# Four more modulation sixths summed on VectorE, and expert weights loaded as 8 KB rows

## The chip, the cores and the metric

The kernel runs on one core of a Trainium2 chip. The metric is the device time of one execution in microseconds. The kernel before takes 947.39 us (median of three executions, 945.4 to 949.32).

## The reference

Two layers work on 256 latent tokens and 256 context tokens of width 1024. Layer 0 mixes by latent attention beside a gated linear recurrence, layer 1 by a Hyena operator with long filters. Each layer is modulated by the conditioning and ends in a mixture of 16 experts, two of them per token. All weights are float32.

```python
for layer in range(DEPTH):
    mod = (silu_c @ ada_w[layer] + ada_b[layer])[:, None, :]
    sh1, sc1, g1, sh2, sc2, g2 = jnp.split(mod, 6, axis=-1)
    h_lat = modulate(rms_norm(x, norm1_g[layer]), sh1, sc1)
    ...
    x = x + g1 * o_lat
    h_lat = modulate(rms_norm(x, norm2_g[layer]), sh2, sc2)
    ...
    x = x + g2 * grouped_moe(h_lat, router_w, router_b, w1, w3, w2)
# grouped_moe, for each expert e of 16
act = jax.nn.silu(h @ w1[e]) * (h @ w3[e])
y = y + gates[..., e:e + 1] * (act @ w2[e])
```

`ada_w[layer]` is 1024 x 6144, so each of the six "sixths" of a layer is a product of a vector of 1024 with a 1024 x 1024 matrix.

## The kernel before, in words

All weights pass through one list of tiles, each 128 partitions x 2048 floats (1 MB). The list is planned at the start (`plan`, `plan_ada`, `moe_tiles`) and loaded in that order by SyncE (`emit`, the load at L219) into a ring of nine buffers `w`, eight buffers `sp` that the mixers also use for their activations, and one to three buffers `x`. A load waits until its buffer's last reader is done. Each of the two mixtures runs over seven passes (`PASSES`): six with two experts and one with four. In a pass the products with w1 and w3 (`up`, L1244) and w2 (`down`, L1272) take most of TensorE's time; between them stand transposes of the activations (`turn`, L1259) and the scatter back to the tokens (`back`, L1289).

A tile of w1 or w3 holds 512 rows of 512 floats: row r of the matrix lies in partition r mod 128, so each partition gets four pieces of 2 KB. A tile of w2 gives each partition two pieces of 4 KB (2 KB for the last pass, whose w2 comes in column halves).

The sixths of the modulation are made in the background by `ada_step`, one of eight row blocks per step, called from the mixer's hand-written sequence `SEQ`, from the attention's list `ATT` and elsewhere. `PLAN` says for each sixth (layer, number) who forms its two column halves. "V" is VectorE: one multiply (L449) and seven multiply-adds over 128 x 512 (L451). "P" is TensorE: eight products with the conditioning as 32-column weights (L442), four at a time in column groups, and a copy on ScalarE (L446). Without an entry a sixth is "VP", one half on each. A finished sixth is turned into columns four steps later (`ada_columns`, transposes at L372, sums at L379 or L381), or into a row spread over the partitions (`ada_row`, L391).

In front of a mixture the router transposes the tokens (`enter`, L576), ScalarE and VectorE write the normalized tokens as a high and a low part (`high`, L627, and `low_`, L633), and TensorE gathers the tokens of each expert from these (L1204, L1215).

The order of each engine's instructions is made by the framework's scheduler from the program order and from its own timing estimates; within the mixtures a few stretches are left as written.

Of the kernel before, what the change touches and what calls it, by code (L numbers as in the profile page):

```python
# [24 lines left out]
STATIC = 4  # L25
DYN = 16 - STATIC
PASSES = ((0, 1), (2, 3), (8, 9), (4, 5, 6, 7), (10, 11), (12, 13), (14, 15))
LAST = len(PASSES) - 1
QUAD = 4
NW = 9  # L30
N8 = 8
# [29 lines left out]
FILLS = 40  # L61
PLAN = {(0, 3): "VV", (1, 2): "VV", (1, 4): "PP", (1, 5): "PP"}
TIN = 0
# [30 lines left out]
def _pack_params(v):  # L94
    pk = np.zeros((128, NPK), np.float32)

    def cols(name, a):
        a = np.asarray(a)
        pk[:a.shape[0], PK[name]:PK[name] + a.shape[1]] = a

    def chunks(a):
        return np.asarray(a).reshape(-1, 128).T

    cols("c", chunks(v["c"]))
    cols("cc", chunks(v["c_ctx"]))
    cols("n1", chunks(v["norm1_g"]))
    cols("n2", chunks(v["norm2_g"]))
# [10 lines left out]
    cols("rw", np.asarray(v["router_w"]).reshape(8, 128, 16).transpose(1, 0, 2).reshape(128, 128))  # L118
    cols("adab", chunks(v["ada_b"]))
# [47 lines left out]
def build(tc, A, dbg=None, stop=None):  # L167
# [43 lines left out]
    def emit(n):  # L211
        for _ in range(n):
            if emitted[0] < len(order):
# [4 lines left out]
                v = t[:shape[0], :shape[1] * shape[2]].rearrange("p (k f) -> p k f", k=shape[1])  # L218
                nc.sync.dma_start(v, src() if callable(src) else src)  # L219
                made[key] = v  # L220
# [51 lines left out]

    def expert(nme, l, e, r0, nk, c0, nf):

        w = A["moe_" + nme]
        if e < STATIC:
            return mat(w[l, e], r0, nk, c0, nf)
        return lambda: mat(w[l, bass.ds(chosen[l][e - STATIC], 1)].rearrange("o k f -> (o k) f"), r0, nk, c0, nf)

    def moe_tiles(l):  # L280
        for j, es_ in enumerate(PASSES):
            for nme in ("w1", "w3"):
                for kk in range(2):
                    for e in es_:
                        yield ((nme, l, e, kk), expert(nme, l, e, kk * 512, 4, 0, 512), (128, 4, 512))
            for h in range(2):
                for e in es_:
                    if j < LAST:
                        yield (("w2", l, e, h), expert("w2", l, e, h * 256, 2, 0, 1024), (128, 2, 1024))
                    elif h == 0:  # L290
                        yield (("w2", l, e, 0), expert("w2", l, e, 0, 4, 0, 512), (128, 4, 512))
            if j == LAST:
                for h in range(2):
                    for e in es_:
                        yield (("w2", l, e, 1 + h), expert("w2", l, e, h * 256, 2, 512, 512), (128, 2, 512))

# [71 lines left out]
    def ada_columns(l, s, hf, use, e, four, n):  # L368

        p2 = ps()  # L370
        for m in range(4):
            T.transpose(p2[:, m * 128:m * 128 + 128], e[:, m * 128:m * 128 + 128], ident)  # L372
        pv = p2.rearrange("p (m q r) -> p m q r", m=4, q=4)
# [165 lines left out]
    def in_order(engines=""):  # L539
# [3 lines left out]
        if engines:  # L543
            manual.append(tc.manual_schedule(engines={ENG[e] for e in engines}))
            manual[0].__enter__()

    class router:

# [22 lines left out]
        def enter(self, i):  # L571
# [3 lines left out]
            for k in range(4):  # L575
                T.transpose(p[:, k * 128:k * 128 + 128], x[:, t, (4 * n + k) * 128:(4 * n + k) * 128 + 128], ident)  # L576
            S.activation(self.alloc().bitcast(BF16)[:, :512], x[:, t, n * 512:n * 512 + 512], AF.Square,
# [45 lines left out]
        def high(self, t):  # L623

            for n in range(2):
                c = slice(n * 512, n * 512 + 512)
                S.activation(self.y[0][:, t, c], x[:, t, c], AF.Copy, scale=self.r[t])  # L627

        def low_(self, t):

            for n in range(2):
                c = slice(n * 512, n * 512 + 512)
                V.scalar_tensor_tensor(self.y[1][:, t, c], x[:, t, c], self.r[t], self.y[0][:, t, c].bitcast(F32),  # L633
                                       op0=OP.mult, op1=OP.subtract)

# [525 lines left out]
    def moe(l, route, ws, filler=None, fills=((0, 0, 0),) * 8, budget=0, late=None, prepare=None, finish=None):  # L1161
# [94 lines left out]
        def turn(j):  # L1256
            p = ps()
            for k in range(4):
                T.transpose(p[:, k * 128:k * 128 + 128], act[j][:, k * 128:k * 128 + 128], ident)  # L1259
            at = act[j] = w2("at")  # L1260
# [53 lines left out]
        def again(nme, e, k, n=0):  # L1314
            t = wk.tile([128, 512], F32, tag="t2", name=nm("wr"), bufs=WT2[l])
            nc.sync.dma_start(t, A["moe_" + nme][l, e, k * 128:k * 128 + 128, n * 512:n * 512 + 512])
            return t
# [9 lines left out]
        next(steps, None)  # L1327
        bg_all()
        route.gates()
# [8 lines left out]
        for j in range(LAST + 1):  # L1338
# [8 lines left out]
            else:  # L1347
                slots(0, gate, firsts)
                slots(1, gate, firsts)
            fill(fills[j][0])  # L1350
            up(j, "w3", first, firsts)
# [421 lines left out]
```

## Time and profile before

| | |
|---|---|
| median of three executions | 947.39 us |
| the profiled execution's own time | 945.29 us |
| its span, first to last instruction | 943.4 us |
| granted TensorE clock, mean | 0.975 |
| TensorE busy | 863.5 us (92%) |
| VectorE busy | 462.8 us (49%) |
| ScalarE busy | 228.9 us (24%) |
| read from HBM | 287.42 MB, 306 GB/s over the span |

Shares of busy time are averages over stages: start (to 45 us), mixer of layer 0 (to 250), mixture 0 (to 530), Hyena mixer (to 690), mixture 1 (to 933) and the end. In the rows PE is TensorE's matrix multiply and PEld its weight load, DVE VectorE, ACT ScalarE, SP SyncE. One float32 product of the program appears in the records as two MATMULs. A busy TensorE isn't one at its peak, since the ends of its instructions are modelled.

### The profile page before, as it was taken

To read this page: it belongs to the slowest core of one execution; us is meant where nothing else is said; L and a number is where in the kernel's file an instruction comes from. 1 tells how busy PE (TensorE), PEld (TensorE's weight loads), DVE (VectorE), ACT (ScalarE), POOL (GpSimd) and SP (SyncE) were. 2 spreads that over 40 slices of the span, in tenths; PEclk is the share of its full clock that TensorE was granted. 3 is DMA by queue.
4 is the path that set the end of the run, shared out by engine and by line. 5 is a ranking of instruction groups with operands and counts; after the bars stand their busy time and mean duration, and the time that the engine had idled before them with its cause. 6 is when DMAs were issued, how large, how long until landed. Compare 5 with 4: busy or idle time off the path is not lost. (4 is left out here: it accounts for less than half of the span.)

```text
span 943.4 us, 10841 instructions
## 1 busy us (share of the span) xinstructions
PE 863.5 (92%) x3976; PEld 447.2 (47%) x3976; DVE 462.8 (49%) x1124; ACT 228.9 (24%) x446; POOL 15.7 (2%) x21
## 2 busy tenths in 40 slices
PE   3998999999999999899998599999989999988984
PEld 2345655574553534333433487776553532423431
DVE  5469785771643454536433648756272323122123
ACT  3276414430411221313122222211031110100112
POOL 0000000000000010101000000000000000000000
PEclk9999999999899999999999799999979999999998
DMA  9957689476799999999999673643199999999993
GB/s 351 353 187 248 224 269 369 165 248 242 244 385 397 329 384 387 395 390 396 396 338 372 229 267 131 223 151 116 57 386 352 389 395 387 404 389 396 396 387 144
DMA packets 130567, 289.33 MB, mean 307 GB/s; under 512 B 6828, under 2 KB 8876, under 8 KB 130500
## 3 DMA queue, kind: packets, MB, share of 16 engines
q1 hardware_dynamic: 129428, 286.39, 82.9%
q10 hardware_dynamic: 1072, 2.10, 0.7%
q8 instruction: 36, 0.59, 0.3%
q14 instruction: 31, 0.25, 0.1%
HBM read 287.42 MB, written 1.05 MB: 306 GB/s over the span
## 5 line engine op out<-in xcount | busy, mean ns | idle before, releaser
L1244 PE MATMUL ps<-w,xe 128*64 128x512 f32 (+1 forms) x696 | 174.6, 597 | 2.4 <-DMA w<-in_moe_w 2.4
L1244 PEld LDWEIGHTS ps<-w,xe 128*64 128x64 f32 (+1 forms) x696 | 50.4, 129 | 87.5 <-issue 79.2
L1272 PE MATMUL ps<-w,at 128*64 128x512 f32 (+1 forms) x344 | 86.0, 597 | 4.5 <-DMA w<-in_moe_w 2.7
L1594 PE MATMUL ps<-xt,w 128*128 128x256 f32 x384 | 87.4, 388 | 1.8 <-ACT xt L1558 1.8
L1594 PEld LDWEIGHTS ps<-xt,w 128*128 128x128 f32 x384 | 74.4, 195 | 14.6 <-ACT xt L1558 2.1
L1291 DVE TENSOR_TENSOR x<-x,ps 128x512 f32<-128x512 f32 x56 | 36.9, 683 | 64.6 <-PE ps L1289 64.6
L1278 DVE SCALAR_TENSOR_TENSOR ye<-ps,gs,grow 128x512 f32<-128x512 f32 x28 | 20.9, 748 | 83.1 <-PE ps L1272 83.1
L1244 PE MATMUL ps<-sp,xe 128*64 128x512 f32 (+1 forms) x216 | 54.5, 598 | 1.4 <-DMA sp<-in_moe_w 1.2
L451 DVE SCALAR_TENSOR_TENSOR e<-w,sg,e 128x512 f32<-128x512 f32 x70 | 51.4, 744 | 3.0 <-DMA w<-in_ada_w 2.3
L1272 PEld LDWEIGHTS ps<-w,at 128*64 128x64 f32 (+1 forms) x344 | 26.7, 130 | 50.6 <-issue 40.0
L1280 ACT ACTIVATE yeh<-ye 128x512 fp32r<-128x512 f32 x28 | 17.6, 630 | 117.5 <-DVE ye L1278 117.5
L1244 PE MATMUL ps<-x,xe 128*64 128x512 f32 (+1 forms) x112 | 37.4, 595 | 1.6 <-DMA x<-in_moe_w 1.6
L1254 DVE TENSOR_TENSOR th<-th,ps 128x512 f32<-128x512 f32 x14 | 9.6, 687 | 59.0 <-PE ps L1244 59.0
L1244 PEld LDWEIGHTS ps<-sp,xe 128*64 128x64 f32 (+1 forms) x216 | 16.7, 132 | 30.0 <-issue 26.3
L1220 ACT ACTIVATE xe<-ps,modc 128x256 f32<-128x256 f32 (+1 forms) x32 | 15.8, 539 | 58.0 <-DVE xe L1218 58.0
L517 PE MATMUL ps<-w,x 128*128 128x512 f32 x64 | 28.4, 595 | 0.7 <-ACT x L1608 0.7
L1249 ACT ACTIVATE th<-ps 128x512 f32<-128x512 f32 x14 | 8.4, 597 | 84.1 <-PE ps L1244 68.5
L835 PE MATMUL ps<-hT,w 128*128 128x512 f32 x64 | 28.0, 593 | 0.4 <-DMA w<-in_ev_w_in 0.4
L517 PE MATMUL ps<-w,mix 128*128 128x512 f32 x64 | 28.2, 594 | 0.0
L1272 PE MATMUL ps<-sp,at 128*64 128x512 f32 (+1 forms) x112 | 26.0, 598 | 2.3 <-ACT at L345 1.7
L442 PE MATMUL ps<-w,cs 128*32 128x512 f32 x160 | 27.1, 714 | 0.0
L930 PE MATMUL ps<-w,hT 128*128 128x288 f32 (+1 forms) x96 | 26.8, 434 | 0.0
(355 smaller groups left out, 1311.0 us busy)
## 6 DMA issues: line engine op xcount, KB each, us to landing
w<-in_moe_w SPq DMA_DIRECT2D x126, 1024.0 KB, 13.9
w<-in_ada_w SPq DMA_DIRECT2D x48, 1024.0 KB, 7.3
sp<-in_moe_w SPq DMA_DIRECT2D x41, 1024.0 KB, 14.6
x<-in_moe_w SPq DMA_DIRECT2D x21, 1024.0 KB, 14.2
w<-in_od_w_in SPq DMA_DIRECT2D x12, 1024.0 KB, 6.8
w<-in_ev_w_in SPq DMA_DIRECT2D x4, 1024.0 KB, 10.9
w<-in_ev_w_out SPq DMA_DIRECT2D x4, 1024.0 KB, 7.9
w<-in_moe_w SPq DMA_DIRECT2D x8, 512.0 KB, 9.8
```

The costliest lines, as they stand in the source:

```text
L442: T.matmul(part[hf][32 * q:32 * q + 32, :], cs[:, k - 3 + q, :], get(("ada", l, s, hf, k // 4))[:, q, :], start=(k == 3), stop=(k == 7), t ...
L451: V.scalar_tensor_tensor(eh, w[hf], c, eh, op0=OP.mult, op1=OP.add)
L517: T.matmul(po[t][n], a[:, k, t * 128:t * 128 + 128], b[:, n * 512:n * 512 + 512], start=(k == korder[0] and i == 0), stop=(k == korder[-1] ...
L835: T.matmul(uxp[b], get(("wux", hf))[:, k % 4, b * 128:b * 128 + 128], hT[hf][:, k % 4, :], start=(k == 0), stop=(k == KD - 1))
L930: T.matmul(p[:, :n], hT[k // 4][:, k % 4, t * 128:t * 128 + 128], get((w, k // 4))[:, k % 4, :], start=(k == 0), stop=(k == KD - 1))
L1220: S.activation(e[:, k, :w], p[:, w:2 * w], AF.Identity, scale=sc[:, k:k + 1], bias=sh[:, k:k + 1])
L1244: T.matmul(p[room * i:room * i + room, :], xe[j // 2][:, k, o:o + room], weight(nme, e, k), start=(k == 0), stop=(k == KD - 1), tile_posit ...
L1272: T.matmul(p[room * i:room * i + room, :], act[j][:, o:o + room], weight("w2", e, k, n), start=(k == 0), stop=(k == 3), tile_position=(0, ...
L1278: V.scalar_tensor_tensor(e, po[j, n], gs[j], grow[l, 5][:, n * 512:n * 512 + 512], op0=OP.mult, op1=OP.mult)
L1280: S.activation(h, e, AF.Copy)
L1291: V.tensor_tensor(xs, xs, p, op=OP.add)
L1594: T.matmul(pb, w[:, k % 4, b * 128:b * 128 + 128], hT[:, k, :], start=(k == 0 and b % 2 == 0), stop=(k == KD - 1 and b % 2 == 1))
```

## The change

It has three parts. `PLAN` now gives both halves of the sixths (0, 2), (0, 4), (0, 5) and (1, 0) to VectorE; before they were "VP". The expert tiles are cut otherwise: a partition takes consecutive rows of the matrix, four of w1 and w3, two of w2, which are 8 KB without a gap (`GROUP`, `expert_rows`). The last pass's w2, a column half, keeps rows of 2 KB, and its tile of four becomes two loads. So that the sums stay the same, everything that meets these tiles is permuted: norm2's gains, the router's weights and the second halves of the biases on the host, the router's transposes and the modulation's column transposes of sixths 3 to 5 with a stride of four floats, the high and low parts read with a stride of four, and `turn` with a stride of two. Last, the call that finishes the open background work (`bg_all`) moves in each mixture from ahead of the gates to behind the first pass's `slots`.

```diff
+GROUP = {"w1": 4, "w3": 4, "w2": 2}
...
-PLAN = {(0, 3): "VV", (1, 2): "VV", (1, 4): "PP", (1, 5): "PP"}
+PLAN = {(0, 2): "VV", (0, 3): "VV", (0, 4): "VV", (0, 5): "VV", (1, 0): "VV", (1, 2): "VV", (1, 4): "PP", (1, 5): "PP"}
...
-                nc.sync.dma_start(v, src() if callable(src) else src)
+                a = src() if callable(src) else src
+                if len(a.shape) == 3:
+                    nc.sync.dma_start(v, a)
+                else:
+                    g = a.shape[2]
+                    for b in range(a.shape[1]):
+                        nc.sync.dma_start(v[:, b * g:b * g + g], a[:, b])
...
+    def expert_rows(w, nme, c0, nf):
+        return w.rearrange("(a p k) f -> p a k f", p=128, k=GROUP[nme])[:, :, :, c0:c0 + nf]
...
-            T.transpose(p2[:, m * 128:m * 128 + 128], e[:, m * 128:m * 128 + 128], ident)
+            T.transpose(p2[:, m * 128:m * 128 + 128], e[:, m * 128:m * 128 + 128] if s < 3 else e[:, m::4], ident)
...
-                T.transpose(p[:, k * 128:k * 128 + 128], x[:, t, (4 * n + k) * 128:(4 * n + k) * 128 + 128], ident)
+                T.transpose(p[:, k * 128:k * 128 + 128], x[:, t, n * 512 + k:n * 512 + 512:4], ident)
...
-                S.activation(self.y[0][:, t, c], x[:, t, c], AF.Copy, scale=self.r[t])
+                S.activation(by_rows(self.y[0][:, t, c]), x[:, t, c].rearrange("p (q k) -> p k q", k=4), AF.Copy,
+                             scale=self.r[t])
...
-                V.scalar_tensor_tensor(self.y[1][:, t, c], x[:, t, c], self.r[t], self.y[0][:, t, c].bitcast(F32),
-                                       op0=OP.mult, op1=OP.subtract)
+                V.scalar_tensor_tensor(by_rows(self.y[1][:, t, c]), x[:, t, c].rearrange("p (q k) -> p k q", k=4),
+                                       self.r[t], by_rows(self.y[0][:, t, c].bitcast(F32)), op0=OP.mult, op1=OP.subtract)
...
-                T.transpose(p[:, k * 128:k * 128 + 128], act[j][:, k * 128:k * 128 + 128], ident)
+                T.transpose(p[:, k * 128:k * 128 + 128], act[j][:, k // 2 * 256 + k % 2:k // 2 * 256 + 256:2], ident)
...
         next(steps, None)
-        bg_all()
         route.gates()
...
                 slots(1, gate, firsts)
+                bg_all()
             fill(fills[j][0])
```

The table shows little of what moves. On VectorE in the mixer, between the features of the queries and the copy of the queries (`qm`), this stands in the kernel before; `e` is the sum of a sixth, `w` a weight tile, `y` the recurrence's gate:

```order
L449 TENSOR_SCALAR e_861<-w_862,sg 128x512
L451 SCALAR_TENSOR_TENSOR e_777<-w_811,sg,e_777 128x512
L451 SCALAR_TENSOR_TENSOR e_861<-w_862,sg,e_861 128x512
L343 COPY vt_708<-ps_855 128x256
L422 SCALAR_TENSOR_TENSOR e_777<-fixed_71,kc,e_777 24x512
L451 SCALAR_TENSOR_TENSOR e_861<-w_862,sg,e_861 128x512 x2
L451 SCALAR_TENSOR_TENSOR e_861<-w_902,sg,e_861 128x512 x4
L422 SCALAR_TENSOR_TENSOR e_861<-fixed_71,kc,e_861 24x512
L974 TENSOR_SCALAR y_99<-y_99 128x1024
L975 TENSOR_TENSOR y_99<-y_99,ug_366 128x1024
L1070 SCALAR_TENSOR_TENSOR y_99<-y_99,ug_366 128x1024
L343 COPY qm_907<-ps_913 128x384
```

And this in the changed kernel, whose lines 467, 438, 994, 995, 1090 and 359 are lines 451, 422, 974, 975, 1070 and 343 of before:

```order
L467 SCALAR_TENSOR_TENSOR e_857<-w_860,sg,e_857 128x512
L438 SCALAR_TENSOR_TENSOR e_775<-fixed_71,kc,e_775 24x512
L467 SCALAR_TENSOR_TENSOR e_857<-w_858,sg,e_857 128x512
L994 TENSOR_SCALAR y_99<-y_99 128x1024
L467 SCALAR_TENSOR_TENSOR e_857<-w_860,sg,e_857 128x512
L467 SCALAR_TENSOR_TENSOR e_857<-w_897,sg,e_857 128x512
L995 TENSOR_TENSOR y_99<-y_99,ug_366 128x1024
L467 SCALAR_TENSOR_TENSOR e_857<-w_860,sg,e_857 128x512
L467 SCALAR_TENSOR_TENSOR e_857<-w_897,sg,e_857 128x512
L467 SCALAR_TENSOR_TENSOR e_857<-w_899,sg,e_857 128x512
L1090 SCALAR_TENSOR_TENSOR y_99<-y_99,ug_366 128x1024
L359 COPY qm_903<-ps_909 128x384
```

The sums of the sixths (0, 2) and (0, 5), `e_775` and `e_857` there, have doubled and now also stand between the gate's steps and ahead of the copy of the queries. In all, 24 of the added operations stand ahead of VectorE's first softmax maximum (L1084 before) and eight between it and the attention's last output (L1113).

On TensorE, where the keys and values (L1004) wait for VectorE's features of the queries, this stands before; L442 are the products of the sixth (0, 2):

```order
L372 MATMUL ps_789<-kc,e_547 128x128 x4
L372 MATMUL ps_797<-kc,e_547 128x128 x4
L442 MATMUL ps_806<-w_784,cs 32x512 x2
L1004 MATMUL ps_749<-w_556,cT_724 128x512
L1004 MATMUL ps_754<-w_556,cT_724 128x512
L442 MATMUL ps_806<-w_784,cs 32x512 x2
L442 MATMUL ps_806<-w_813,cs 32x512 x4
L958 MATMUL ps_818<-kc,cqn_774 128x128
```

In the changed kernel (lines 388, 1024 and 978 are 372, 1004 and 958):

```order
L388 MATMUL ps_790<-kc,e_547 128x128 x4
L388 MATMUL ps_798<-kc,e_547 128x128 x4
L1024 MATMUL ps_747<-w_556,cT_722 128x512
L1024 MATMUL ps_752<-w_556,cT_722 128x512
L978 MATMUL ps_817<-kc,cqn_772 128x128
```

The eight products are gone, as in three more places of the mixer, and the transposes of `cqn` stand right behind the work that waits for nothing new.

On SyncE the loads keep their order but for a few buffers; each expert tile, `128x4x512` or `128x2x1024` before, is one load of `128x2048`, and each layer has four loads more, for the last pass's w2.

## Rows read from the trace of the kernel before

**Rows 1.** The page: busy us and share of each engine
```profile
PE 863.5 (92%) x3976; PEld 447.2 (47%) x3976; DVE 462.8 (49%) x1124; ACT 228.9 (24%) x446; POOL 15.7 (2%) x21
```
**Rows 2.** Stretches: start:end, length, busy per engine (count), clock, DMA share, GB/s
```profile
100.00:167.00 67.00, 67.00 (x289) 39.84 (x288) 49.60 (x126) 20.39 (x43) 0.00 (x0) 1.00 0.84 298
167.00:213.00 46.00, 44.75 (x294) 29.60 (x292) 35.48 (x85) 19.47 (x47) 0.00 (x0) 1.00 0.59 204
...
250.00:530.00 280.00, 258.60 (x1249) 111.67 (x1242) 129.31 (x336) 61.88 (x126) 13.71 (x16) 0.98 1.02 378
700.00:930.00 230.00, 213.16 (x1022) 85.79 (x1021) 64.01 (x142) 28.81 (x58) 0.00 (x0) 0.99 1.01 382
```
**Rows 3.** Waits of TensorE, whole span: for whom, us in total, times, longest
```profile
PE ps L1272 <- DMA w<-in_moe_w: 2.7, 4, 0.7
...
PE ps L1244 <- DMA w<-in_moe_w: 2.4, 2, 1.5
...
PE ps L1244 <- DMA x<-in_moe_w: 1.6, 1, 1.6
...
PE ps L1244 <- DMA sp<-in_moe_w: 1.2, 1, 1.2
...
PE ps L1272 <- DMA sp<-in_moe_w: 0.6, 1, 0.6
```
**Rows 4.** TensorE in order of time, from 380 us: the first of these waits
```profile
386.47 0.63 PE L1244 MATMUL ps<-w,xe 128*32 128x512 f32 x3 [1.51 <-DMA w<-in_moe_w]
```
**Rows 5.** Two stretches of mixture 1, columns as in rows 2
```profile
720.00:730.00 10.00, 8.65 (x44) 2.95 (x42) 1.11 (x2) 0.38 (x1) 0.00 (x0) 1.00 1.03 411
735.00:750.00 15.00, 15.00 (x64) 5.77 (x61) 5.25 (x9) 1.23 (x2) 0.00 (x0) 1.00 1.05 387
```
**Rows 6.** The page: DMA issues, KB each, median us to landing
```profile
w<-in_moe_w SPq DMA_DIRECT2D x126, 1024.0 KB, 13.9
...
sp<-in_moe_w SPq DMA_DIRECT2D x41, 1024.0 KB, 14.6
x<-in_moe_w SPq DMA_DIRECT2D x21, 1024.0 KB, 14.2
```
**Rows 7.** TensorE in order of time around one group of L442: start, us
```profile
100.93 1.07 PE L442 MATMUL ps<-w,cs 128*32 128x512 f32 x8
101.93 7.17 PE L966 MATMUL ps<-hT,w 128*128 128x256 f32 x32
```
**Rows 8.** VectorE: L451 from 100 to 167 us, and four in a row
```profile
L451 DVE SCALAR_TENSOR_TENSOR e<-w,sg,e 128x512 f32<-128x512 f32 x16 | 11.8, 746 | 0.3
...
71.89 2.73 DVE L451 SCALAR_TENSOR_TENSOR e<-w,sg,e 128x512 f32<-128x512 f32 x4
```
**Rows 9.** Two of VectorE's waits from 100 to 167 us
```profile
DVE cT L959 <- PE ps L958: 3.3, 1, 3.3
...
DVE rs L481 <- ACT junk L933: 1.9, 1, 1.9
```
**Rows 10.** VectorE in order of time, 92 to 100 us, with its idle time
```profile
93.21 1.22 DVE L903 SCALAR_TENSOR_TENSOR a<-a,th 128x1024 f32<-128x1024 f32 x1 [0.85 <-ACT a L901]
...
97.65 1.54 DVE L451 SCALAR_TENSOR_TENSOR e<-w,sg,e 128x512 f32<-128x512 f32 x2 [2.08 <-DMA w<-in_ada_w]
```
**Rows 11.** Single lines: ns min/median/max, first and last start, form
```profile
L1619 PEld LDWEIGHTS ps<-kc,u x32: 194/207/210, 556.1 to 612.9; 128*128 128x128 f32 x32
...
L576 PEld LDWEIGHTS ps<-kc,x x32: 139/141/226, 242.2 to 686.5; 128*128 128x128 f32 x32
...
L1684 DVE TENSOR_TENSOR x<-x,ps x4: 674/683/689, 647.9 to 664.5; 128x512 f32<-128x512 f32 x4
...
L1291 DVE TENSOR_TENSOR x<-x,ps x56: 672/680/689, 297.2 to 933.1; 128x512 f32<-128x512 f32 x56
...
L627 ACT ACTIVATE yh<-x,rs x8: 706/707/722, 247.9 to 690.0; 128x512 fp32r<-128x512 f32 x8
...
L633 DVE SCALAR_TENSOR_TENSOR yl<-x,rs,yh x8: 743/745/747, 253.7 to 700.2; 128x512 fp32r<-128x512 f32 x8
```

More of the change, by code (lines that the diff above doesn't have):

```diff
@@ L102, in chunks, with by_rows @@
         return np.asarray(a).reshape(-1, 128).T
+    def by_rows(a):
+        return np.asarray(a).reshape(-1, 128, 4).transpose(1, 0, 2).reshape(128, -1)
     cols("c", chunks(v["c"]))
@@ L106, in _pack_params @@
     cols("n1", chunks(v["norm1_g"]))
-    cols("n2", chunks(v["norm2_g"]))
+    cols("n2", by_rows(v["norm2_g"]))
     cols("qn", chunks(v["mla_q_norm_g"]))
@@ L117, in _pack_params @@
     cols("rb", np.broadcast_to(np.asarray(v["router_b"])[None, :], (128, 16)))
-    cols("rw", np.asarray(v["router_w"]).reshape(8, 128, 16).transpose(1, 0, 2).reshape(128, 128))
-    cols("adab", chunks(v["ada_b"]))
+    cols("rw", np.asarray(v["router_w"]).reshape(2, 128, 4, 16).transpose(1, 0, 2, 3).reshape(128, 128))
+    ab = np.asarray(v["ada_b"]).reshape(2, 6, 1024)
+    cols("adab", np.concatenate([(chunks if s < 3 else by_rows)(ab[l, s]) for l in range(2) for s in range(6)], axis=1))
     cols("dec", chunks(v["hy_decay"]))
@@ L271, in plan_moe, with expert @@
                 plan(key, src, shape)
-    def expert(nme, l, e, r0, nk, c0, nf):
+    def expert_rows(w, nme, c0, nf):
+        return w.rearrange("(a p k) f -> p a k f", p=128, k=GROUP[nme])[:, :, :, c0:c0 + nf]
+    def expert(nme, l, e, a0, na, c0, nf):
         w = A["moe_" + nme]
         if e < STATIC:
-            return mat(w[l, e], r0, nk, c0, nf)
-        return lambda: mat(w[l, bass.ds(chosen[l][e - STATIC], 1)].rearrange("o k f -> (o k) f"), r0, nk, c0, nf)
+            return expert_rows(w[l, e], nme, c0, nf)[:, a0:a0 + na]
+        return lambda: expert_rows(w[l, bass.ds(chosen[l][e - STATIC], 1)].rearrange("o k f -> (o k) f"), nme, c0, nf)[:, a0:a0 + na]
     def moe_tiles(l):
@@ L284, in moe_tiles @@
                     for e in es_:
-                        yield ((nme, l, e, kk), expert(nme, l, e, kk * 512, 4, 0, 512), (128, 4, 512))
+                        yield ((nme, l, e, kk), expert(nme, l, e, kk, 1, 0, 512), (128, 4, 512))
             for h in range(2):
@@ L288, in moe_tiles @@
                     if j < LAST:
-                        yield (("w2", l, e, h), expert("w2", l, e, h * 256, 2, 0, 1024), (128, 2, 1024))
+                        yield (("w2", l, e, h), expert("w2", l, e, h, 1, 0, 1024), (128, 2, 1024))
                     elif h == 0:
-                        yield (("w2", l, e, 0), expert("w2", l, e, 0, 4, 0, 512), (128, 4, 512))
+                        yield (("w2", l, e, 0), expert("w2", l, e, 0, 2, 0, 512), (128, 4, 512))
             if j == LAST:
@@ L294, in moe_tiles @@
                     for e in es_:
-                        yield (("w2", l, e, 1 + h), expert("w2", l, e, h * 256, 2, 512, 512), (128, 2, 512))
+                        yield (("w2", l, e, 1 + h), expert("w2", l, e, h, 1, 512, 512), (128, 2, 512))
     plan_moe(0)
@@ L545, in in_order, with by_rows @@
             manual[0].__enter__()
+    def by_rows(v):
+        return v.rearrange("p (k q) -> p k q", k=4)
     class router:
@@ L1315, in again @@
             t = wk.tile([128, 512], F32, tag="t2", name=nm("wr"), bufs=WT2[l])
-            nc.sync.dma_start(t, A["moe_" + nme][l, e, k * 128:k * 128 + 128, n * 512:n * 512 + 512])
+            g = GROUP[nme]
+            nc.sync.dma_start(t, expert_rows(A["moe_" + nme][l, e], nme, n * 512, 512)[:, k // g, k % g])
             return t
```

## The prediction

> **What bounds the kernel now.** I read the page first: TensorE is busy 863.5 of 943.4 us, VectorE 462.8 [rows 1]. These are means over stages, so the next view is the table of stretches [rows 2]. In the mixer from 100 to 167 us TensorE has no idle time at all (67.00 of 67), VectorE 17.4 us; in the attention from 167 to 213 TensorE is busy 44.75 of 46 and VectorE 35.48. In both mixtures the DMA engines are as full as they get (share 1.02 and 1.01, at 378 and 382 GB/s) while TensorE is idle 21.4 and 16.8 us. Full DMA engines alone cost nothing: the third view, TensorE's waits, says how much of that idle time ended with a weight tile landing. It is 2.7 + 2.4 + 1.6 + 1.2 + 0.6 = 8.5 us in nine waits [rows 3]. So TensorE bounds the mixer, and for all but 8.5 us the mixtures.
>
> The profiled execution took 945.29 us, 2.1 below the median of 947.39. The sum is made against 945.3, and 2 is added at the end. Half a per cent, 4.7 us, is about what a measurement of this kernel can tell from no change.
>
> **Part 1, four halves from TensorE to VectorE.** TensorE loses eight groups of four products, two per sixth. One stands at 100.93 and the next work starts at 101.93, so a group holds TensorE 1.0 us (its modelled length is 1.07) [rows 7]: 8 x 1.0 = 8 us less, 6 of it ahead of the first softmax, 2 inside the attention. ScalarE loses one short copy per sixth; it is busy 20.39 of 67 us there [rows 2], so that is worth nothing.
>
> VectorE gains 32 operations of 128x512. A multiply-add takes 746 ns on the mean, but four in a row take 2.73 us, 0.68 each [rows 8]: 32 x 0.68 = 21.8 us, at the mean 32 x 0.746 = 23.9. By the order of the change 24 come ahead of the first softmax maximum, 8 behind it.
>
> - Up to the softmax, 24 x 0.68 = 16.3 us are added. VectorE has 49.6 us of work in the 67 us of that stretch. Its waits of 3.3 us for the product L958 and of 1.9 us for ScalarE [rows 9] stand ahead of the first added sum's operations in the new order, so these 5.2 us can't be filled. Ahead of 100 us it is idle 0.85 + 2.08 = 2.9 us [rows 10], room for four operations (2.7 us). VectorE then needs 49.6 + 16.3 + 5.2 - 2.7 = 68.4 us, TensorE 67.0 - 6 = 61. VectorE becomes the later of the two by little: +1.4 us in place of -6.
> - In the attention VectorE needs 35.5 + 8 x 0.68 = 40.9 us, TensorE 44.75 - 2 = 42.75. Both fit; but softmax alternates between them, and I take half of the 2 us: -1.
>
> Part 1 is 1.4 - 1 = 0.4, about 0. Its bounds are -8 (VectorE's work is all hidden, TensorE's saving all kept) and +23.9 (nothing hidden). I take 0, since the fill is nearly exact.
>
> **Part 2, rows of 8 KB.** A mixture loads 94 tiles of 1 MB, 188 in all [rows 6]. In a stretch in which mostly w2 with its 4 KB rows arrives, the full DMA engines move 411 GB/s; where mostly w1 and w3 arrive in 2 KB rows, 387 [rows 5]. Sixteen engines then take 2048 x 16 / 387 = 84.7 ns for a row of 2 KB and 4096 x 16 / 411 = 159.5 for one of 4 KB: 74.8 ns per 2 KB and 9.9 ns per row. By that line a row of 8 KB takes 309 ns, an estimate of 424 GB/s; the bounds are 411, the best rate seen there, and the straight-line 438 of 2048 x 16 / 74.8. A tile takes 2.47 us in place of 2.71 (w1, w3) or 2.55 (w2), about 0.19 us less on the mean. TensorE's first late tile is at 386.47 us [rows 4]; at 378 GB/s [rows 2] the queue has brought (386 - 250) x 378 / 1049 = 49 tiles of 1,049 KB since 250 us: a lead of 49 x 0.19 = 9.3 us against a longest single wait of 1.6 [rows 3]; even at 411 GB/s the 2 KB tiles gain 0.16 us each, a lead near 5 us. Both cover the waits, so all 8.5 us go. Nothing comes on top, since TensorE's own 258.6 and 213.2 us [rows 2] are untouched; the rest of the saving becomes idle time of the queue. Bounds: 0 (same rate) and -12 (the waits behind a late tile shrink as well). Next in line is TensorE itself.
>
> The tile of the last pass's w2 that becomes two loads adds four issues per layer on SP, whose queue is full of transfers and not of issues: 0. A load that finishes later holds what follows by no more than half of one tile's 2.7 us, which the lead covers.
>
> **Part 3, the strides.** Transposes that read every second float load their weights in 207 ns against 141 for contiguous ones, while VectorE reading every second float takes 683 against 680 [rows 11]. No row shows a stride of four. Bounds: nothing at all, and twice the time of everything touched: 8 x 0.707 = 5.7 us on ScalarE, 8 x 0.745 = 6.0 on VectorE, and 32 router transposes and 32 column transposes (two layers, sixths 3 and 4, eight each) x 0.141 = 9.0 us of weight loads. I take the nearest row, the weight load's 66 ns: 64 x 0.066 = 4.2 us, of which a third shows, since loads run beside products: +1.5. For `turn` with a stride of two the same 66 ns lie behind products of the neighbouring experts, which keep TensorE's queue filled, and behind the idle time that waits leave: 0.
>
> VectorE's row shows no price for a stride of two, and none for four. [...]
>
> **The moved call.** `bg_all` in front of the gates issues the last transposes and rows of the modulation (L372, L391); behind the first pass's slots they are the same instructions. What it no longer delays are the gates; what it now could delay are the first products of pass one, by the same instructions: 0.
>
> **Sum:** 945.3 + 0 - 8.5 + 1.5 = 938.3; with the 2 to the median, **940 us**.
>
> **Rivals.**
>
> *VectorE becomes the mixer's bound.* If the idle time can't be filled, because the sums' tiles land late or because an added operation stands ahead of the gate's step (L974 and L1070 of before) or of the copy of the queries that TensorE waits for, the queue grows. The decision is how much of the 21.8 us finds a gap: below some 15 us filled, the mixer grows by more than the 7 us that part 2 leaves over. With a third filled it grows by 16: 945.3 + 16 - 8.5 + 1.5 = 954, median 956, slower. For it: the new sums stand between the gate's steps. Against: 17.4 and 10.5 us of idle time lie in just these stretches [rows 2]. Chance 0.13.
>
> *The long rows aren't faster.* If the 24 GB/s between the two stretches [rows 5] come from something other than the rows (what else is in the queue, HBM), the lead never grows: 945.3 + 1.5 = 946.8, median 949, no change. Against it: it is the only thing that differs between these tiles, and the DMA share is above 1 in both. Chance 0.10. [...]
>
> *Stride four is dear.* L627 and L633 stand between mixer and mixture, where TensorE waits for little else. If they take twice as long, 5.7 + 6.0, some 12 us: with half of it on the path 938.3 - 1.5 + 6 = 942.8, median 945, no change; with all of it 948.8, median 951. Chance 0.14, since the weight loads show that a stride can cost, and VectorE's row that it need not. [...]
>
> *The mixer keeps its 8 us.* If VectorE's additions all find gaps, earlier ones included (the first sums can start before 88 us): 945.3 - 8 - 8.5 + 1.5 = 930.3, median 932. Chance 0.13.
>
> The forecast itself has 0.50.
>
> **Range and chances.** The main case by itself runs from 935 to 945 (part 2 from -12 to -4, part 1 by 2 either way). The range of 929 to 951 adds the second rival, the third and the fourth; outside lie the first rival (0.13) and the ends of the others, 0.2 in all. Faster by over half a per cent (below 942.7): the forecast, less a tenth of the chance for its weak end (0.45), the fourth rival (0.13) and part of the third (0.04), 0.62. Slower (above 952.1): the first rival and the dearest end of the third, 0.15. The rest, 0.23, is no change.
>
> **What would show it.** In the table of stretches for both mixtures, 420 GB/s or more while the DMA share is 1, and slices with a share below 1; among TensorE's waits, those for expert tiles near 0. The first softmax maximum stays near 167 us and the mixer's end within 1 us. L627 and L633 stay at 707 and 745 ns. The prediction is wrong if the first softmax moves later by 5 us or more, if loads of 8 KB rows land no faster, or if the expert waits go and other idle time of TensorE in the mixtures takes their place.

## The result, and the profile after

The changed kernel takes 931.42 us (median of four, 929.54 to 932.53) against 947.06 us of the kernel before: the ratio is 0.983, with a 95% interval of 0.981 to 0.985. Two later comparisons of the same two kernels gave 0.984 [0.981, 0.987] and 0.987 [0.985, 0.989]. The forecast was 940 us. The sign is right and the time lies inside the range, but the gain is 15.6 us where 7.4 were forecast: more than twice as much.

The profiled execution of the changed kernel took 929.54 us, 15.75 less than that of before. Where it went is read by following the same product through both traces:

| TensorE starts | before, us | after, us | after minus before |
|---|---|---|---|
| last stretch of the mixer's output (L517, now L533) | 229.70 | 230.05 | +0.35 |
| products with w1 run on in mixture 0 (L1443, now L1464) | 280.48 | 281.80 | +1.32 |
| end of mixture 0's four-expert pass (L1289, now L1309) | 411.52 | 409.58 | -1.94 |
| router of layer 1 (L589, now L608) | 684.75 | 682.84 | -1.91 |
| four-expert pass of mixture 1, ahead of its w2 | 811.72 | 808.28 | -3.44 |
| first product after the late tiles of that mixture | 868.72 | 854.81 | -13.91 |
| last product | 931.99 | 916.20 | -15.79 |

From the products with w1 on, mixture 0 gains 3.3 us (from +1.32 to -1.94), mixture 1 13.9 (from -1.91 to -15.79), and there one stretch of 57 us stands out. The mixer of layer 0 (+0.35) and the Hyena mixer (+0.03) contribute nothing. The page's first row answers to [rows 1]:

```profile
PE 846.0 (91%) x3912; PEld 447.3 (48%) x3912; DVE 483.9 (52%) x1156; ACT 229.4 (25%) x442; POOL 15.7 (2%) x21
```

TensorE's busy time fell by 17.5 us; the products taken from it are 8 of these, by the forecast's 1.0 us per group. VectorE's rose by 21.1, close to the 32 x 0.68 = 21.8 of the forecast. The stretches of [rows 2] and [rows 5], in the changed kernel (start:end, length, busy time per engine, clock, DMA share, GB/s):

```profile
100.00:167.00 67.00, 59.70 (x230) 37.81 (x229) 60.16 (x144) 17.75 (x40) 0.00 (x0) 0.97 0.70 253
167.00:213.00 46.00, 43.42 (x277) 30.13 (x275) 40.20 (x95) 18.24 (x46) 0.00 (x0) 0.96 0.71 249
```
```profile
718.00:728.00 10.00, 8.71 (x44) 3.07 (x41) 1.11 (x2) 0.38 (x1) 0.00 (x0) 1.00 1.00 420
733.00:748.00 15.00, 15.00 (x65) 5.93 (x62) 5.32 (x9) 1.23 (x2) 0.00 (x0) 1.00 1.01 422
```

The rows of 8 KB run at 420 to 422 GB/s (424 were estimated), w1, w3 and w2 alike. And TensorE's waits for expert tiles over the whole span, the answer to the 8.5 us of [rows 3], are 1.6 us:

```profile
PE ps L1292 <- DMA w<-in_moe_w: 1.2, 2, 0.6
PE ps L1264 <- DMA x<-in_moe_w: 0.4, 1, 0.4
```

So waits of 6.9 us went, and the mixtures became some 17 us shorter. Most of the other 10 us stand in no row of waits. They are in TensorE's busy time: here is the stretch of mixture 1 between the same two products, first before, then after, with nearly the same records (219 and 220).

```profile
811.72:868.72 57.00, 48.65 (x219) 15.22 (x213) 13.48 (x23) 5.71 (x11) 0.00 (x0) 1.00 1.04 397
```
```profile
808.28:854.81 46.53, 41.56 (x220) 15.46 (x213) 13.46 (x23) 5.70 (x11) 0.00 (x0) 1.00 1.01 421
```

Of the 10.47 us, 3.38 are idle time and 7.09 are TensorE being "busy" for less time with the same work at the same clock. The timeline of the products with w2 in that pass shows how. Before:

```profile
817.52 6.30 PE L1272 MATMUL ps<-sp,at 128*32 128x512 f32 x36 [0.73 <-ACT at L345]
824.41 1.90 PE L1272 MATMUL ps<-sp,at 128*32 128x512 f32 x4 [0.58 <-DMA sp<-in_moe_w]
826.97 1.90 PE L1272 MATMUL ps<-w,at 128*32 128x512 f32 x4 [0.65 <-DMA w<-in_moe_w]
829.53 0.62 PE L1272 MATMUL ps<-w,at 128*32 128x512 f32 x1 [0.66 <-DMA w<-in_moe_w]
...
833.08 1.07 PE L1244 MATMUL ps<-w,xe 128*64 128x512 f32 x2
```

After, where no product waits for a tile:

```profile
814.08 4.08 PE L1292 MATMUL ps<-sp,at 128*32 128x512 f32 x34 [0.64 <-ACT at L361]
817.57 0.86 PE L1292 MATMUL ps<-w,at 128*32 128x512 f32 x2
...
820.58 0.85 PE L1292 MATMUL ps<-w,at 128*32 128x512 f32 x2
821.37 1.07 PE L1264 MATMUL ps<-w,xe 128*64 128x512 f32 x2
```

Four experts with 32 tokens each stand in four column groups of TensorE, and their products run side by side: 34 records in 4.08 us, 0.12 each. Before, the last tiles came one by one, 2.56 us apart (824.41, 826.97, 829.53), which for 1,049 KB is 410 GB/s, the pace of the stream. At two of these places TensorE held the four records of one tile, alone, for 1.90 us: 0.475 each, busy all the while. The same 64 records take 15.56 us before (817.52 to 833.08) and 7.29 after; these are differences of starts and don't depend on the modelled ends. Of the 8.27 us of difference the table of waits shows 0.58 + 0.65 + 0.66 = 1.9.

The strides cost what the rows of before couldn't show. Lines 595, 646 and 653 are the router's transposes, the high and the low part (L576, L627 and L633 of [rows 11]):

```profile
L595 PEld LDWEIGHTS ps<-kc,x x32: 195/210/262, 242.6 to 684.7; 128*128 128x128 f32 x32
...
L646 ACT ACTIVATE yh<-x,rs x8: 1195/1209/1251, 248.4 to 689.3; 128x512 fp32r<-128x512 f32 x8
...
L653 DVE SCALAR_TENSOR_TENSOR yl<-x,rs,yh x8: 1122/1142/1161, 254.5 to 697.9; 128x512 fp32r<-128x512 f32 x8
```

### The profile page after: what moved, and what is told of

Same layout as the page of the kernel before. It is cut to its first block, busy times and chain, and to the rows that moved or that the text cites. A ratio compares the mean times of both kernels' runs of the same rounds, so it can differ in the third digit from the quotient of the medians.

```text
span 927.7 us, 10761 instructions
## 1 busy us (share of the span) xinstructions
PE 846.0 (91%) x3912; PEld 447.3 (48%) x3912; DVE 483.9 (52%) x1156; ACT 229.4 (25%) x442; POOL 15.7 (2%) x21
## 5 line engine op out<-in xcount | busy, mean ns | idle before, releaser
L1264 PE MATMUL ps<-w,xe 128*64 128x512 f32 (+1 forms) x696 | 171.9, 596 | 0.0
L1615 PEld LDWEIGHTS ps<-xt,w 128*128 128x128 f32 x384 | 74.0, 194 | 14.4 <-ACT xt L1579 2.1
L467 DVE SCALAR_TENSOR_TENSOR e<-w,sg,e 128x512 f32<-128x512 f32 x98 | 70.7, 743 | 0.5
L533 PE MATMUL ps<-w,x 128*128 128x512 f32 x64 | 28.4, 595 | 0.7 <-ACT x L1629 0.7
L533 PE MATMUL ps<-w,mix 128*128 128x512 f32 x64 | 28.2, 594 | 0.0
L950 PE MATMUL ps<-w,hT 128*128 128x288 f32 (+1 forms) x96 | 28.2, 453 | 0.0
L1302 DVE TENSOR_TENSOR yel<-ye,yeh 128x512 fp32r<-128x512 f32 x28 | 19.3, 691 | 14.8 <-ACT yeh L1300 10.5
L1309 PE MATMUL ps<-yeh,st 128*128 128x512 f32 x56 | 21.7, 433 | 4.8 <-ACT yeh L1300 4.8
```

The lines of the kernel that those rows point to most:

```text
L467: V.scalar_tensor_tensor(eh, w[hf], c, eh, op0=OP.mult, op1=OP.add)
L533: T.matmul(po[t][n], a[:, k, t * 128:t * 128 + 128], b[:, n * 512:n * 512 + 512], start=(k == korder[0] and i == 0), stop=(k == korder[-1] ...
L950: T.matmul(p[:, :n], hT[k // 4][:, k % 4, t * 128:t * 128 + 128], get((w, k // 4))[:, k % 4, :], start=(k == 0), stop=(k == KD - 1))
L1264: T.matmul(p[room * i:room * i + room, :], xe[j // 2][:, k, o:o + room], weight(nme, e, k), start=(k == 0), stop=(k == KD - 1), tile_posit ...
L1302: V.tensor_tensor(o, e, h.bitcast(F32), op=OP.subtract)
L1309: T.matmul(p, st[j][:, t * 128:t * 128 + 128], ye[j, n][i], start=(i == 0), stop=(i == 1))
```

## The experiments

Each kernel was measured side by side with the kernel before; ratios below 1 are faster.

### Is it the rows, or the products taken from TensorE?

There was a rival in the forecast that gave 932 us, close to the measured 931.42: the mixer keeps its 8 us and the rows bring the visible 8.5 (theory P). Theory L says that late tiles cost more than their waits and the mixer gives nothing. *old_rows* takes the long rows out of the changed kernel and leaves everything else:

```diff
-        return w.rearrange("(a p k) f -> p a k f", p=128, k=GROUP[nme])[:, :, :, c0:c0 + nf]
+        return w.rearrange("(a k p) f -> p a k f", p=128, k=GROUP[nme])[:, :, :, c0:c0 + nf]
```

> The changed kernel with one load per tile as it is now, but each partition takes every 128th row of the matrix again, pieces of 2 KB (w1, w3) and 4 KB (w2) as before; strides, PLAN, permuted parameters and the moved call stay, so the weights meet the wrong rows of the activations. Theory L (late tiles): 385 to 411 GB/s, all late tiles are back, 945 to 950 us, that is 0.998 to 1.005 of the time before. Theory P (PLAN): 938 to 941 us, 0.992.

Measured: 947.09 us, ratio 1.001 [0.999, 1.003]. The whole net gain is gone. Its stretches are those of [rows 5] again, and the four-expert pass takes 819.32 to 834.96, 15.64 us, with its tiles one by one:

```profile
720.00:730.00 10.00, 8.71 (x42) 3.04 (x40) 1.11 (x2) 0.38 (x1) 0.00 (x0) 1.00 1.04 408
735.00:750.00 15.00, 15.00 (x68) 5.81 (x64) 4.59 (x7) 1.85 (x3) 0.00 (x0) 1.00 1.05 387
```
```profile
819.32 6.37 PE L1292 MATMUL ps<-sp,at 128*32 128x512 f32 x36 [0.64 <-ACT at L361]
826.29 1.90 PE L1292 MATMUL ps<-sp,at 128*32 128x512 f32 x4 [0.60 <-DMA sp<-in_moe_w]
828.85 1.90 PE L1292 MATMUL ps<-w,at 128*32 128x512 f32 x4 [0.66 <-DMA w<-in_moe_w]
...
834.96 1.07 PE L1264 MATMUL ps<-w,xe 128*64 128x512 f32 x2
```

*plan_only* is the kernel before with the new `PLAN`, *rows_only* the changed kernel with the old one.

```diff
-PLAN = {(0, 3): "VV", (1, 2): "VV", (1, 4): "PP", (1, 5): "PP"}
+PLAN = {(0, 2): "VV", (0, 3): "VV", (0, 4): "VV", (0, 5): "VV", (1, 0): "VV", (1, 2): "VV", (1, 4): "PP", (1, 5): "PP"}
```

> The kernel before with the new PLAN alone. Theory L: TensorE's 8 us turn into waits for VectorE's sums, 945 to 949 us, with waits of some 4 us for ckvn and 1.5 us for e in TensorE's table. Theory P: 938 to 940 us.

Measured: 945.9 us, 1.000 [0.998, 1.002]. The waits that were expected are in TensorE's table from 80 to 215 us; in the kernel before that table has only the L889 row and one of 1.2 us for `pm`:

```profile
PE ps L958 <- DVE ckvn L942: 4.1, 1, 4.1
PE ps L889 <- ACT th L896: 2.9, 1, 2.9
PE ps L1096 <- ACT pm L1086: 2.2, 2, 1.9
PE ps L391 <- DVE e L422: 1.7, 2, 1.5
PE ps L1004 <- ACT junk L933: 0.8, 1, 0.8
```

> The changed kernel with the old PLAN (the sixths (0, 2), (0, 4), (0, 5) and (1, 0) are VP again); long rows, strides and the moved call stay. Theory L (late tiles): the whole gain of some 15.6 us comes from expert tiles that are no longer late, because a late tile costs TensorE more than the idle time ahead of its first product: 930 to 934 us. Theory P (plan): the forecast's 8.5 us for the rows were right and the other 7 to 8 us are TensorE's products taken out of the mixer: 938 to 940 us.

Measured: 933.52 us, 0.988 [0.985, 0.991]. Theory P is out by this run and by the two above. The changed kernel had 0.983 in the first measurement, beside other executions of the kernel before, so what `PLAN` is worth beside the rows stayed open; *after_again* is the changed kernel as it is.

> The changed kernel unchanged, beside the variants of this call. The first comparison gave 0.983 of the time before, the old PLAN with the long rows 0.988. If PLAN is worth nothing beside the rows, this comes out at 0.986 to 0.988; if it is worth some 4 us where TensorE has weights to work on, at 0.981 to 0.985.

Measured: 931.22 us, 0.984 [0.981, 0.987]: the value lies in the case in which `PLAN` is worth 4 us, the interval reaches into the other. Two kernels measured side by side decide it, *after_third* and *rows_again* (the same files as after_again and rows_only):

> The changed kernel once more, as the common base of this call: 0.983 to 0.985.

> The changed kernel with the old PLAN again, this time beside the changed kernel itself. If PLAN is worth 4 us beside the long rows, 0.987 to 0.989 and above the changed kernel's interval's middle by 0.004; if the earlier difference was between calls, within 0.002 of the changed kernel.

Measured: 931.95 us, 0.987 [0.985, 0.989] and 932.54 us, 0.987 [0.985, 0.988]. The first lies above what was expected of it, and the two can't be told apart: `PLAN` is worth nothing beside the rows either, and the earlier difference lay between measurements. *rows_strict* has the long rows and strides alone, with the old `PLAN` and the old place of the moved call:

> Long rows and strides alone: old PLAN, old place of the call. If the parts add up (PLAN 4 us, move 4 us, rows the rest), 0.991 to 0.993; if the rows carry everything, 0.984 to 0.986.

Measured: 935.43 us, 0.989 [0.988, 0.991]: 10.0 of the 13.5 us that the changed kernel (after_third) gains beside it, between the two cases that were expected. The two small parts together bring the remaining 0.002 of the ratio, which the intervals don't separate from nothing.

### Do late tiles cost that much?

If they do, then a kernel with the short rows but fewer tiles must gain as well. *fewer_before* leaves out w3 of experts 0 to 3 in the kernel before and uses w1 there.

```diff
+                        if nme == "w3" and e in SHARED:
+                            continue
...
+            if nme == "w3" and e in SHARED:
+                nme = "w1"
```

> The kernel before, which leaves out w3 of experts 0 to 3 in both layers and uses their w1 in its place: eight tiles of 1 MB less ahead of the four-expert pass, some 21 us of queue time per mixture, with rows of 2 and 4 KB as before. Theory L: no tile is late any more, 930 to 934 us without any long row. If late tiles cost only the 8.5 us of visible waits: 937 to 940 us.

Measured: 937.28 us, 0.992 [0.989, 0.994], the visible price and no more. But in its list every later tile had moved to another buffer, and it still waited 8.1 us for tiles, in other places. *skip_before* drops the same eight loads per layer and leaves every other tile in its buffer:

```diff
+                if key[0] == "w3" and key[2] in SHARED:
+                    made[key] = made[("w1",) + key[1:]]
...
+                    continue
```

> The kernel before without the loads of w3 of experts 0 to 3 (their w1 is used in its place), with every other tile in the buffer that it has in the kernel before: the run before this one had shifted all buffers and still waited 8 us for tiles. Theory L: with 21 us of queue time less ahead of the four-expert pass no tile is late, 0.983 to 0.988. If late tiles cost only their visible 8.5 us: 0.991 to 0.993.

Measured: 940.23 us, 0.994 [0.991, 0.996]. Theory L as I had put it fails here: 21 us of transfers less in each mixture, and tiles are late as before, 9.0 us of waits in all. The stretch ahead of the four-expert pass of mixture 1, first of this kernel, then of the kernel before:

```profile
720.00:780.00 60.00, 56.89 (x272) 24.91 (x272) 19.08 (x38) 7.67 (x15) 0.00 (x0) 1.00 0.85 311
```
```profile
720.00:780.00 60.00, 58.11 (x278) 24.90 (x274) 17.97 (x36) 7.28 (x14) 0.00 (x0) 1.00 1.04 395
```

With less to load the DMA engines stood still (share 0.85): the buffers were full, and SyncE's loads waited for their readers, 34.2 us for products with w2 alone between 690 and 770 us. What is saved ahead of the pass can't be kept for it beyond the ring. So the eight tiles were taken out at the place where they are missed, *skip_late*, with `SHARED = (4, 5, 6, 7)` in the same edit:

> The kernel before without the loads of w3 of experts 4 to 7, the four-expert pass itself (their w1 is used in its place; 8 tiles per layer, every other tile in its own buffer, rows of 2 and 4 KB). The eight tiles of experts 0 to 3 gave 0.9935, and in that trace the DMA engines stood idle from the full ring of buffers ahead of the pass (311 GB/s, share 0.85): lead that is won early is not carried on. Theory S (stream): from the four-expert pass to its end mixture 1 runs at the pace of the weight stream, and TensorE's busy time there holds products that trickle in with their tiles; the same 21 us less of it at this place give the whole of the gain, 0.981 to 0.986, with TensorE's busy time in mixture 1 some 8 to 10 us lower. If only the visible waits can go: 0.991 to 0.993.

Measured: 922.65 us, 0.977 [0.975, 0.979], faster than theory S said and than the changed kernel, with rows of 2 and 4 KB. The products with w2 of the four-expert pass run four abreast, 7.85 us from 802.48 to 810.33:

```profile
802.48 4.08 PE L1280 MATMUL ps<-sp,at 128*32 128x512 f32 x34 [0.53 <-ACT at L353]
...
808.98 1.42 PE L1280 MATMUL ps<-w,at 128*32 128x512 f32 x3
810.33 1.07 PE L1252 MATMUL ps<-w,xe 128*64 128x512 f32 x2
```

TensorE's busy time over the whole span fell by 18.7 us against [rows 1], with the same 3976 records:

```profile
PE 844.8 (92%) x3976; PEld 441.7 (48%) x3976; DVE 464.3 (50%) x1124; ACT 229.2 (25%) x446; POOL 15.3 (2%) x21
```

Eight tiles per layer gave 6 us ahead of the pass and 22 in it. The 22 are those of both mixtures, 42 us of stream in all. Followed as in the table above, mixture 0 gains 9.4 us (from 280.48 to 281.88 at its products with w1, from 411.52 to 403.48 at the end of its pass), mixture 1 14.4 (from 684.16 to 676.09 at the router, from 931.99 to 909.48 at the end): 7.7 of these in the products with w2 of the pass, 7.0 ahead of them, nothing behind. That more than the changed kernel's gain came out fits: eight tiles at 2.6 us are 21 us of stream at one place, while the long rows save some 0.2 us per tile all along it.

*pieces_2k* was to bring the short pieces back into the changed kernel with its layout kept, in two loads per tile:

```diff
-                        nc.sync.dma_start(v[:, b * g:b * g + g], a[:, b])
+                        for y in range(2):
+                            h = slice(b * g + y, b * g + g, 2)
+                            nc.sync.dma_start(v[:, h], a[:, b, y::2])
```

> The changed kernel, but each expert tile comes in two loads whose pieces are 2 KB (w1, w3: every second piece of a partition's 8 KB per load) or 4 KB (w2); layout, strides, PLAN and the moved call stay. Theory L: the rate in the mixtures falls back to 385 to 411 GB/s, the late tiles return, 944 to 949 us. Theory P: half the gain stays, 939 to 941 us. A third theory, that the order of loads or the moved call made the gain and not the rate: 931 to 933 us.

Measured: 955.63 us, 1.012 [1.009, 1.015]; no theory had it slower than before. It isn't the control it was meant to be: SyncE's queue waits 113.6 us for earlier loads into `w`, against 8.7 in the kernel before and 55.2 in the changed one. What these waits cost was not tried. old_rows is the cleaner run. The first row of SyncE's waits:

```profile
SPq L233 <- DMA w<-in_moe_w: 113.6, 174, 3.6
```

### What VectorE does with the four sixths

In the changed kernel TensorE waits 4.13 us for `ckvn`, behind the sums of the sixth (0, 4), which VectorE makes among the gate's scans. *no04* gives half of that sixth back to TensorE:

```diff
-PLAN = {(0, 2): "VV", (0, 3): "VV", (0, 4): "VV", (0, 5): "VV", ...
+PLAN = {(0, 2): "VV", (0, 3): "VV", (0, 5): "VV", ...
```

> The changed kernel with the sixth (0, 4) as VP again. Its sums stand between the gate's scans and ahead of ckvn, for which TensorE waits 4.1 us in the changed kernel at 115 us and not at all before. If VectorE's queue is what keeps TensorE's saving from showing: 2 us of products back, 4 us of wait gone, 2 us below the changed kernel. If something else takes that wait's place: the same or 1 to 2 us above it.

Measured: 926.94 us, 0.981 [0.978, 0.984], beside after_again (931.22): 4 us by the medians, the intervals overlap. The place in the changed kernel and then in no04 (lines 950, 978: products of the recurrence's input, transposes of `ckvn`):

```profile
105.90 5.32 PE L950 MATMUL ps<-w,hT 128*128 128x384 f32 x16
115.36 0.41 PE L978 MATMUL ps<-kc,ckvn 128*128 128x128 f32 x2 [4.13 <-DVE ckvn L962]
```
```profile
109.96 5.43 PE L950 MATMUL ps<-w,hT 128*128 128x384 f32 x16
115.23 0.38 PE L978 MATMUL ps<-kc,ckvn 128*128 128x128 f32 x2
```

The transposes start at the same time, with the same records of L950 done by then: the changed kernel is 4.1 us ahead at L950 and gives this away in the wait. The 4 us of no04 are won behind it. Two stretches hold the same products in both kernels, the 16 records of L950 that follow and, behind a wait of 1.9 us that both have, four of the attention's (L1103); first the changed kernel, then no04:

```profile
115.60:122.46 6.86, 6.86 (x19) 3.74 (x17) 1.86 (x15) 1.06 (x5) 0.00 (x0) 0.75 0.47 148
170.10:173.21 3.11, 3.11 (x6) 1.08 (x5) 1.05 (x4) 1.68 (x6) 0.00 (x0) 0.55 0.95 353
```
```profile
115.44:121.26 5.82, 5.82 (x24) 3.66 (x23) 1.61 (x3) 0.57 (x2) 0.00 (x0) 1.00 0.30 84
166.71:168.42 1.71, 1.71 (x6) 0.71 (x5) 0.82 (x3) 1.67 (x6) 0.00 (x0) 1.00 1.04 392
```

In the changed kernel TensorE stood still for 4.13 and for 1.91 us, and behind each wait its granted clock was lower for some microseconds, 0.75 and 0.55 on the mean of these stretches. That is 1.7 us (L950 alone takes 5.2 in no04, whose stretch holds six records of L978 besides) and 1.4. Two short waits, 0.78 for L1024 and 0.54 for `cqn`, are also gone in no04: together 4.4 of the 4.8 us by which no04 is ahead at the mixer's end. The clock varies: in no04 it stays at 1.00 behind the same 1.9 us of wait, and in after_again at 1.00 behind a wait of 3.11 for `ckvn`. So how much of the 4 us belongs to this sixth stays open.

> The changed kernel with the sixths (0, 4) and (0, 2) as VP again; (0, 5) and (1, 0) stay on VectorE. Without (0, 4) alone the time was 4 us below the changed kernel. TensorE still waits 1.7 us there for the last two sums of a sixth that becomes a row (e at 145 us). If (0, 2) is that one and blocks more than the 2 us of products that it saves, 0 to 1 us lower than without (0, 4) alone; if it saves its products, 2 us higher.

Measured: 926.75 us, 0.981 [0.979, 0.983]: the same as without (0, 4) alone. The sum of (0, 2) on VectorE and its products on TensorE cost alike.

### The strides and the moved call

```diff
-                S.activation(by_rows(self.y[0][:, t, c]), x[:, t, c].rearrange("p (q k) -> p k q", k=4), AF.Copy,
+                S.activation(by_rows(self.y[0][:, t, c]).rearrange("p k q -> p q k"), x[:, t, c].rearrange("p (q k) -> p q k", k=4), AF.Copy,
```

> Without (0, 4), and ScalarE's high parts read the tokens in order and write with a stride of 128 floats in place of reading with a stride of four. In the changed kernel each takes 1.21 us in place of 0.71. If only the strided read costs: 0.71 us again, mixture 0 begins up to 0.5 us earlier, which the time can't tell. If a strided write costs as much or more: 1.2 us or more, same time or 1 us above.

Measured: 925.24 us, 0.979 [0.977, 0.982]. A stride on the writing side costs ScalarE almost the same, 1.17 us against 1.21; the time can't tell the two kernels apart. Of the versions that compute everything this one has the lowest median, and by their medians it and no04 lie below both kernels of the case.

> Without (0, 4), and the call that finishes the background work stands ahead of the gates again, as before. If the move is worth nothing: within 1 us of the kernel without (0, 4) alone. If the work delays the gates and with them the gather: mixture 0's first products 1 to 2 us later.

```diff
         next(steps, None)
+        bg_all()
         route.gates()
...
                 slots(1, gate, firsts)
-                bg_all()
```

Measured: 931.71 us, 0.986 [0.983, 0.988], 6.5 us above no04_wr beside it (0.979 [0.977, 0.982]) and 5 above no04's median, where the forecast had the move at nothing. In the traces no04_bg is 5.1 us later at the first transposes of mixture 0's activations (282.52 and 277.39), but 1.6 of these are there at 88 us already (L909, 88.44 and 86.85), long ahead of the moved call; its start ran at a granted clock of 0.86 from 20 to 45 us, no04's at 1.00. Some 3.5 us arise at the gather. With the call in its old place the transposes of a sixth (L388) stand in the middle of the gather (L1224) and wait for ScalarE's copy; in no04 the gather runs through. First no04_bg, then no04:

```profile
255.53 1.47 PE L1224 MATMUL ps<-P,yh 128*128 128x256 f32 x8 [2.80 <-DVE P L1211]
258.90 1.98 PE L388 MATMUL ps<-kc,e 128*128 128x128 f32 x8 [1.90 <-ACT e L462]
260.53 2.06 PE L1224 MATMUL ps<-P,yh 128*128 128x256 f32 x8
```
```profile
253.91 3.33 PE L1224 MATMUL ps<-P,yh 128*128 128x256 f32 x16 [2.80 <-DVE P L1211]
257.04 2.19 PE L1224 MATMUL ps<-P,yl 128*128 128x256 f32 x14
```

ScalarE's copy is late because a load that ScalarE issues stands ahead of it in its order:

```profile
256.93 0.47 ACTq L1458 DMA_DIRECT2D w<-in_hy_w  x1
257.45 0.91 ACT L1467 ACTIVATE e<-fixed,ndec 128x256 f32<-128x256 f32 x2 [6.73 <-DMA sp<-in_moe_w]
258.27 1.06 ACT L462 ACTIVATE e<-ps 128x512 f32<-128x512 f32 x2
```

In the changed kernel, with (0, 4) on VectorE, one of the two copies stands ahead of that load (253.96 us) and nothing waits. *bg_old* is the changed kernel with the old place:

> The changed kernel with the old place of the call that finishes the background work. Without (0, 4) the move was worth 4.6 us. If that is the move's own worth, 0.988 to 0.989 here; if it depended on that PLAN, as the changed kernel.

Measured: 930.86 us, 0.985 [0.984, 0.987], the changed kernel's own time. There too one copy stands ahead of the load (255.06 us), and the transposes in the gather (260.38) wait for nothing. So the move is worth nothing in the change as made, and some 3.5 us by the traces in a kernel whose scheduler happens to order ScalarE the other way.

## Why the prediction was wrong in its size

**What bounds the kernel.** "TensorE bounds the mixer, and for all but 8.5 us the mixtures": right for the mixer and for mixture 0 ahead of its four-expert pass. Wrong for the four-expert passes, of mixture 1 above all: there the weight stream sets the pace (DMA share 1.04 for the whole stretch of 57 us, and 21 us less of the stream at this place in each mixture give 9.4 and 14.4 us).

**Part 1, the four halves: right.** Forecast 0, measured 1.000 alone and no difference beside the rows. The bookkeeping held as well: VectorE's first softmax maximum stands at 167.0 us (166.9 before), TensorE's 67 us of work became 59.7 with waits in place of the rest. What I had not placed is the wait itself: it came at `ckvn`, ahead of the queries, and behind it the same products ran at a lower granted clock, so that TensorE's saving went in part into waits and in part into slower products. A quarter less of this part (no04) seems to gain what the whole of it gives away. That these came out even is luck: the forecast had no term for the clock.

**Part 2, the rows: the failed step.** The rate was right (420 to 422 GB/s for 424), the waits went (6.9 of 8.5 us). The step that failed is "Nothing comes on top, since TensorE's own 258.6 and 213.2 us are untouched". TensorE's busy time in the mixtures isn't its own: products of four experts that run abreast when their tiles are there run one by one as tiles trickle in, and count as busy (34 records in 4.08 us after; before, the four records of one tile in 1.90). The term was 8.5 us by the forecast, with -12 as its bound; by the traces it is 17.1 us: 3.3 in mixture 0 from 280.48 to 411.52 and 13.9 in mixture 1, of which one stretch of 57 us holds 3.4 us of idle and 7.1 of busy time. With 17.1 in place of 8.5 and the 1.3 us by which mixture 0 begins later in place of 1.5, the forecast's sum gives 929.5; the profiled execution took 929.54.

"A lead of 49 x 0.19 = 9.3 us" adds up what is saved since 250 us. In mixture 0 it doesn't add up like this: the DMA share falls to 0.80 from 300 to 320 us and 0.84 from 320 to 340, the buffers being full (SyncE's loads wait 33.5 us for products with w2 from 280 to 360 us), and waits of 1.2 us for w2 remain in its four-expert pass. In mixture 1 it does. Here is the way from its router to the long stretch, before and after:

```profile
684.75:811.72 126.97, 119.37 (x639) 54.81 (x641) 47.16 (x150) 21.27 (x43) 0.00 (x0) 0.96 1.02 383
682.84:808.28 125.44, 120.43 (x639) 56.72 (x642) 48.34 (x150) 23.24 (x43) 0.00 (x0) 0.95 1.00 413
```

That is 48.6 MB before and 51.8 after, 3 MB or three tiles more ahead of the stretch, and in the stretch itself 22.6 and 19.6. At 421 GB/s three tiles are 7.2 us; the faster rate alone would shorten the stretch by 3.2 (57 x 397 / 421 = 53.8). By this estimate two thirds of the 10.5 us are lead, one third the rate in the pass.

The tiles of the last pass's w2 added two loads per layer, not four (200 expert loads in the trace for 196); the term was 0 and stays so.

**Part 3, the strides: the size right, the mechanism half.** Loads at a stride of four take 210 ns, as at two (207) and against 141: the row that I took. But the engines pay as well, and the sign that L627 and L633 stay at 707 and 745 ns failed: 0.707 became 1.209 us on ScalarE and 0.745 became 1.142 on VectorE. The third rival put its price on twice the time; it was 1.7 and 1.5 times. Little of it shows: at mixture 0's start TensorE is 1.0 us later by the table above (+0.35 to +1.32, with the moved call in the same stretch), and old_rows, with all strides, is at 1.001. The forecast had +1.5. On VectorE a stride of two floats is free in [rows 11] (683 ns against 680), a stride of four is not (1142 against 745). ScalarE pays for the stride of four (1209 ns against 707); no run has it at two. For TensorE's weight loads the trace goes another way: two floats (207 ns) already cost as much as four (210).

**The moved call:** 0 was right for this change (bg_old), and not in general (no04_bg).

**The rivals.** VectorE as a costly bound didn't happen, since the saved and the added time came out even (its 16 us are two thirds of the 23.9 of the bound, not of the 21.8 that it names, which give 14.5). "The long rows aren't faster" is out by the rate. "The mixer keeps its 8 us" gave the right total for the wrong reason: without the experiments its 932 us would have looked confirmed.

## What to carry to other kernels

A wait for a tile ends in the table of waits only as long as the engine stands still (1.9 of the 8.27 us here); where several tiles feed products that should run side by side, look at how many records run per microsecond and compare the stretch with one in which all tiles are there, before taking busy time for work. Ask of every saved transfer whether the buffers can hold the lead until the place where it is needed: a ring that is full ahead of the bottleneck turns savings there into idle DMA engines (share 0.85 in skip_before). Moving work from a full engine to an emptier one gains only if its place in the other's order isn't ahead of what the first waits for (plan_only: 4.1 us of wait for `ckvn`, ratio 1.000); look also at the granted clock behind such a wait (0.75 behind 4.13 us in the changed kernel), and try the pieces one by one.

## What the runs showed that I had not expected

- Eight tiles per layer less gave 6 us at one place (0.994) and 22 at another (0.977).
- Behind a wait of 4.13 us TensorE's granted clock fell to 0.75 on the mean of the next 6.86 us, and the same products took 1.7 us longer.
- Two loads of 0.5 MB for each tile, in pieces of 2 and 4 KB, made the kernel 1.2% slower than the kernel before (1.012), where single loads with such pieces were level with it (old_rows, 1.001). SyncE's queue waited longer for earlier transfers; what limits it there was not tried further.
- ScalarE takes 1.17 us for 128x512 when it writes with a stride of 128 floats in groups of four, 1.21 when it reads with a stride of four, 0.71 without a stride.
